# A Fourier and Hyena encoder layer on one core: data sums of the gates and of the last projection made beside the filters, weight-sum transfers one per convolution step, eight plain gate products

## The chip, the cores and the metric

The kernel runs on one core of one Trainium2 chip. The metric is the device time of one execution in microseconds, lower is better. PE is the matrix engine, DVE and ACT the vector and scalar engines, POOL the general engine, which also issues one kind of DMA, SP the engine that issues most DMAs. PSUM is the memory that PE writes, SBUF the working memory.

## What is computed

Two sequences (prompt and sample, b = 0 and 1), each 1024 positions by 1024 channels, go through the same layer, all in float32:

```python
xn = rmsnorm(x, g_pre)
fv, fg, hv, hg, mg = split(xn @ w_in)            # 8 sections of 1024 columns
fz = real(fft2 of fv over positions and groups of 256 channels)
y_f = (fz * silu(fg)) @ w_fourier_out
v, x1, x2 = split(short_conv(hv))                # width 3, per channel
z = v
for n, gate in enumerate((x1, x2)):
    z = gate * long_conv(z, filter[n])           # by FFT; filters from a small network
y_h = (z * silu(hg)) @ w_hyena_out
g_f, g_h = split(sigmoid(mg + b_merge))
out = (g_f * y_f + g_h * y_h) @ w_out
return x + rmsnorm(out, g_post)
```

The kernel keeps float32 accuracy by splitting each operand of a product into a rounded part h (made on ACT) and a remainder l (a subtraction on DVE or POOL), and by three matmuls per product: h.h, h.l, l.h (`split`, L167; `mm3`, L469; `times`, L1108).

## The kernel before

**Stages.** The Fourier branch comes first (`phase_fourier`, L601), for b = 0 and then b = 1. It also writes the normalized input of both sequences, transposed, to DRAM (`d_x`, eight blocks of 128 x 1024 each). Then `phase_main` (L986) makes 16 Hyena filters, two per block of 128 channels (`filter_taps`, `filter_spectrum`), and writes their spectra to `d_k`. Beside the filters PE gets plain gate products of b = 0 (`spill_gate`, L876), spread over the 16 filter steps by the list `fill`. Then `branches` (L1034) runs 32 convolution steps, 16 per sequence: the input product of the step (`inproj`, L838), a forward transform, the product with the spectrum, an inverse transform (`conv_back`, tables `cinv`), and the gating product on DVE (`gate`, L980), whose result is z. `phase_tail` (L1147) does what is left: gates of b = 1, the two output networks of both sequences, and the last projection with the norm.

**Plain and block products.** A plain product of 128 columns is 48 matmuls of 512 columns. `inproj` loads the weights in halves, ACT makes wh and POOL makes wl (L854), both with three buffers; for b = 1 the split weights of three sections come back from DRAM. In the tail, products go two column blocks at a time by a Strassen-like scheme with seven block products of 12 matmuls instead of eight (`PH`, L1254). For this it needs sums of weight blocks (A: 11, 12, s1 to s4, 22) and sums of data blocks (Y: B11, B21, B22 plain, T1 to T4 sums). `part2` (L1528) gives the order within a job: 11, 12 (in `first`, L1218), then s2 x T2, s3 x T3, s1 x T1, then 11 and 12 of the next job, s4 x B22, 22 x T4.

**Which gates are plain.** `PLAIN` (L1123) lists ten (section, column block) pairs of b = 1 that are done plainly: six during the last four convolution steps (L1094), and the rest after the last inverse transform (L1103, held behind `self.ended`, the last pT matmul). All other gates of b = 1 become block jobs of two column blocks, eleven of them (`gates`, L1153).

**The data sums.** At the start of the tail's gates (L1509 to L1518) the blocks of `d_x[1]` are loaded again into the raw tile (two buffers, L1511), three DVE operations per pair of row blocks make T1 to T4, and 16 splits round them. The sums of `w_out` for the last projection are made during gate jobs 2 to 5 by `last_sums` (L1241), on POOL and DVE, and stored in `d_t`; `load_sum` and `round_z` (L1399, L1404) fetch and round them at the end of the networks. A copy of `w_out` is made by eight DRAM-to-DRAM transfers on SP (L1524) to `d_wo`, from which `load_own` (L1392) reads the blocks B11, B21, B22.

**The weight sums.** `weight_sums` (L1125) makes the seven weight combinations of both networks in DRAM with 22 transfers on POOL; nine of them add into their destination (`accum_op=ADD`), and must wait for the transfer before. `front` (L1048) issues two per step, from step 2 on.

**Order of work.** The framework's planner orders the instructions of each engine by priority (order in the code) on a modelled timeline, so an instruction without a dependency may be issued much earlier than its place in the code. `issue_after(ins)` keeps the instructions of a block behind `ins` on the engine of `ins`. In the networks and at their end, functions are queued with due times in matmul-group steps (`at(t, f, ...)`, L1367; 28 steps per network, four networks), and `step` runs what is due.

**Rooms.** Memory of a stage is reused by the next one as its tiles come free. The four T tiles (16 KB per partition each) lie where the convolutions' tiles were.

Of the kernel before, what the change touches and what calls it, by code (L numbers as in the profile page):

```python
# [160 lines left out]
class K:  # L161
# [34 lines left out]
    def setup(self, ctx):  # L196
# [30 lines left out]
        self.d_t = [[dt(f"d_t{j}_{k}", [P, 512]) for k in range(4)] for j in range(4)]  # L227
# [758 lines left out]
    def phase_main(self, nct=8, nb=NB, nf=16):  # L986
        tc, nc, a = self.tc, self.nc, self.a
        with ExitStack() as es:
# [25 lines left out]
            rates = self.filter_rates(1, 0, ws)  # L1014
            for i in range(nf):
                nxt = self.filter_taps((i + 1) % 2, (i + 1) // 2, rates, ws) if i + 1 < nf else None
                self.filter_spectrum(i % 2, i // 2, taps, ws)
                if i + 2 < nf:
                    rates = self.filter_rates(i % 2, i // 2 + 1, ws, self.rounded)
                taps = nxt  # L1020
                for sec, c in fill[i * len(fill) // nf:(i + 1) * len(fill) // nf]:
                    self.spill_gate(0, sec, c, ws)
                if i == 2:
                    self.cinv = mi.tile([P, 2, INVW], F32R, name="cinv")
                    self.cin0 = mi.tile([P, 4 * P], F32, name="cin0")
                    nc.sync.dma_start(self.cin0, a["c_in0"])
                if i in (2, 4, 6):

                    s = slice((2, 4, 6).index(i) * INVW // 3, ((2, 4, 6).index(i) + 1) * INVW // 3)
                    nc.gpsimd.dma_start(self.cinv[:, :, s], a["c_inv"][:, :, s])  # L1030
            self.sums_due = list(self.weight_sums())
            self.branches(nb, nct, ws)

    def branches(self, nb, nct, ws):  # L1034
# [49 lines left out]
        for i, (b, n, c) in enumerate(steps):  # L1084
# [38 lines left out]
    PLAIN = [(5, 0), (5, 1), (6, 0), (6, 1), (5, 2), (5, 3), (6, 2), (6, 3), (5, 4), (5, 5)]  # L1123

    def weight_sums(self):  # L1125

        nc, a = self.nc, self.a
        out = []
        for n, w in enumerate(("w_fo", "w_ho")):
            v = a[w].rearrange("(j i) p (h c) -> i h p j c", i=2, h=2)  # L1130
            d = self.d_s[n]
            load = lambda p, src, d=d: out.append(lambda: nc.gpsimd.dma_start(d[p], src))
            more = lambda p, src, d=d: out.append(lambda: nc.gpsimd.dma_start(d[p], src, accum_op=ADD))
# [10 lines left out]
            more(4, v[0, 1])  # L1144
        return out

    def phase_tail(self):  # L1147
# [10 lines left out]
        with ExitStack() as es:  # L1158
# [7 lines left out]
            def prepare(nm, s, c):  # L1166
# [50 lines left out]

            def first(A, Y):  # L1218
                pa, pb = self.psum("mm", 4, "pg"), self.psum("X", 2, "pg")
# [21 lines left out]
            def last_sums(k):  # L1241
                ra, rb = [cell(xp, f"x1{2 * (k % 2) + i}", f"ws{i}") for i in range(2)]
                for r, kk in ((ra, k), (rb, 4 + k)):
                    nc.sync.dma_start(flat(r), a["w_out"][kk * P:(kk + 1) * P])
                self.sub("pool", ra[:, 0], ra[:, 0], ra[:, 1])
                self.sub("pool", ra[:, 1], ra[:, 1], rb[:, 1])
                self.stt("dve", rb[:, 1], ra[:, 0], -1.0, rb[:, 1], MUL, SUB)
                self.add("pool", rb[:, 0], rb[:, 1], rb[:, 0])
                for j, t in enumerate((ra[:, 0], rb[:, 1], ra[:, 1], rb[:, 0])):
                    nc.sync.dma_start(self.d_t[j][k], t)  # L1250
# [31 lines left out]
            def block(g, i):  # L1282
# [8 lines left out]
                if i == 0:  # L1291
                    blocks[g] = gs.tile([P, 2, 4, 512], F32R, tag=ROOM[(g - 1) % 4], name="n", bufs=1)
# [105 lines left out]

            def load_sum(nm):  # L1399
                t = Z[nm] = gs.tile([P, 2, 4, 512], F32R, tag=nm, name=f"o{nm}", bufs=1)  # L1400
                for k in range(4):
                    nc.sync.dma_start(t[:, 1, k].bitcast(F32), self.d_t[int(nm[1]) - 1][k])

            def round_z(nm, k):  # L1404
# [3 lines left out]
                else:  # L1408
                    v = t[:, 1, 2 * k:2 * k + 2]
                    self.split(t[:, 0, 2 * k:2 * k + 2], v, v.bitcast(F32), "dve", "act")  # L1410
            for nm, room, t in (("B21", "x1{}", 88), ("B11", "x0{}", 98), ("B22", "x1{}", 110)):
                at(t, load_own, nm, room)
            at(100, load_sum, "T4")
            at(104, load_sum, "T2")
            at(108, load_sum, "T3")
            for k in range(4):
                at(92 + k, round_z, "B21", k)
                at(100 + k, round_z, "B11", k)
            for k in range(2):
                at(103 + k, round_z, "T4", k)  # L1420
                at(107 + k, round_z, "T2", k)
# [86 lines left out]
            order = ("T2", "T3", "T1", "T4")  # L1508
            T = {j: gs.tile([P, 2, 4, 512], F32R, tag=j, name=j, bufs=1) for j in order}  # L1509
            for k in range(4):  # L1510
                r = gr.tile([P, 4, 512], F32, tag="raw", name="xraw", bufs=2)  # L1511
                for i in range(2):
                    nc.sync.dma_start(flat(r[:, 2 * i:2 * i + 2]), self.d_x[1][k + 4 * i])
                self.sub("dve", r[:, 0:2], r[:, 0:2], r[:, 1::2])
                self.stt("dve", r[:, 3], r[:, 0], -1.0, r[:, 3], MUL, SUB)
                self.add("dve", r[:, 2], r[:, 3], r[:, 2])
                for j, q in zip(order, (3, 1, 0, 2)):
                    self.split(T[j][:, 0, k], T[j][:, 1, k], r[:, q], "dve", "act")  # L1518
            pairs = lambda z: [(t[:, 0], t[:, 1]) for t in z]
            quad = lambda t: [(t[:, 0, k], t[:, 1, k]) for k in range(4)]  # L1520
            for j in order:
                Y[j] = quad(T[j])
            for k in range(8):
                nc.sync.dma_start(self.d_wo[k], a["w_out"][k * P:(k + 1) * P])  # L1524
# [15 lines left out]
            pa, pb, m1 = first(A, Y)  # L1540
            for i, job in enumerate(gates):
# [43 lines left out]
            Y["T1"] = quad(Z["T1"])  # L1585
# [111 lines left out]
```

## Time and profile before

| what | us |
|---|---|
| median of 3 runs | 2380.61 (2377.27 to 2382.72) |
| the profiled execution, its own time | 2382.25 |
| span of the profiled execution, first to last instruction | 2380.5 |
| PE busy | 2330.1 |
| DVE busy | 1973.3 |
| ACT busy | 1115.5 |
| POOL busy | 430.7 |

All stretches and starts are microseconds from the start of the span. The filters run from 254 to 692, the convolutions of b = 0 to about 1089 and of b = 1 to 1643, the last plain products to 1688, the gate jobs to about 1900, the networks to 2213, the output rows to the end. A busy PE isn't PE at its peak: matmuls overlap, so the pace is read from the starts. In the chain of waits and in the rows of a timeline, what stands in brackets is the engine's idle time ahead of the instruction and what ended it.

### The profile page before, as it was taken

What the parts mean: (1) busy time and instruction counts of PE and PEld (TensorE: products, weight loads), DVE (VectorE), ACT (ScalarE), POOL (GpSimd) and SP (SyncE); (2) the same over time, 40 slices, a digit from 0 to 9 for tenths busy, and PEclk for the clock granted to TensorE, in tenths of its full rate; (3) what the DMA queues carried; (4) which work ended last, traced back from release to release, by engine and by line L of the source; (5) the groups of instructions that cost most, each with busy time, mean ns of one, the idle gap of its engine ahead of it and who ended that gap; (6) DMA issues with size and microseconds to landing.
All of it is one profiled execution on the core that took longest, in us unless ns stands there. A gap on an engine that the chain in (4) does not pass through costs nothing.

```text
span 2380.5 us, 36106 instructions
## 1 busy us (share of the span) xinstructions
PE 2330.1 (98%) x12796; PEld 2022.8 (85%) x12796; DVE 1973.3 (83%) x3416; ACT 1115.5 (47%) x2083; POOL 430.7 (18%) x406
## 2 busy tenths in 40 slices
PE   6999999999999999999999999999999999999998
PEld 5999888888888888888889888888788888888786
DVE  7775688878889999999889999997765578778987
ACT  6555667776753333334222332323444365557443
POOL 2342322222243333221000000111300000101211
PEclk9999999999999999999999999999999999999999
DMA  9646655555578787745444444445754688988644
GB/s 318 207 148 220 189 175 166 166 178 171 176 261 272 244 251 231 222 149 195 153 147 133 133 142 144 140 142 177 264 186 161 217 267 272 262 310 258 174 160 142
DMA packets 241888, 471.31 MB, mean 198 GB/s; under 512 B 24103, under 2 KB 81801, under 8 KB 241387
## 3 DMA queue, kind: packets, MB, share of 16 engines
q1 hardware_dynamic: 217949, 398.06, 51.0%
q0 software_dynamic: 23536, 70.91, 10.4%
q8 instruction: 101, 1.65, 0.3%
q14 instruction: 81, 0.66, 0.1%
q10 hardware_dynamic: 221, 0.04, 0.0%
HBM read 322.63 MB, written 173.54 MB: 208 GB/s over the span
## 4 chain that ended last, share of the span: by engine, by line
PE 52%; DVE 3%; DMA 3%; issue 1%; ACT 0%; SPq 0%; DVEq 0%; POOL 0%; POOLq 0%; ACTq 0%
PE pin L193 17%; PE pg L193 14%; PE pn L193 10%; PE pT L193 5%; PE pX L193 5%; DMA d_m<-gt 1%; PE tph L904 1%; DMA xraw<-d_x 1%; DMA d_sh<-x 0%; DVE gt L180 0%; DMA g<-d_g 0%; DVE T L180 0%; DVE wl L180 0%; DVE xraw L180 0%; DVE r L180 0%
## 5 line engine op out<-in xcount | busy, mean ns | idle before, releaser
L193 PE MATMUL pin<-x,wh 128*128 128x512 f32 x2880 | 909.8, 391 | 2.5 <-ACT ktmp L794 2.4
L193 PEld LDWEIGHTS pin<-x,wh 128*128 128x128 f32 x2880 | 534.3, 188 | 103.4 <-ACT ktmp L794 2.6
L193 PE MATMUL pin<-x,wl 128*128 128x512 f32 x1440 | 563.2, 391 | 0.0
L180 POOL TENSOR_TENSOR wl<-wr,wh 128x512 fp32r<-128x512 f32 x132 | 224.2, 1699 | 1104.5 <-ACT wh L170 668.6
L193 PEld LDWEIGHTS pin<-x,wl 128*128 128x128 f32 x1440 | 271.0, 188 | 50.8
L193 PE MATMUL pn<-n,wh 128*128 128x512 f32 x896 | 276.4, 389 | 0.1
L193 PEld LDWEIGHTS pn<-n,wh 128*128 128x128 f32 x896 | 168.1, 188 | 35.8 <-DVE n L180 0.5
L193 PE MATMUL pn<-n,wl 128*128 128x512 f32 x448 | 174.6, 390 | 1.6 <-DVE wl L180 1.5
L180 DVE TENSOR_TENSOR t<-pX,k 128x1024 f32<-128x1024 f32 x128 | 155.4, 1214 | 8.7 <-DMA k<-d_k 5.9
L193 PE MATMUL pX<-bh,cfwd 128*128 128x256 f32 x768 | 162.4, 288 | 0.0
L193 PE MATMUL pT<-cinv,yh 128*128 128x256 f32 x768 | 146.0, 284 | 0.3 <-DVE T0s L180 0.3
L170 ACT CAST wh<-wr 128x512 fp32r<-128x512 f32 x132 | 81.6, 618 | 132.2 <-PE pin L193 90.3
L170 ACT CAST bh<-b 128x512 fp32r<-128x512 f32 x144 | 88.4, 619 | 99.3 <-DVE b L180 73.7
L193 PEld LDWEIGHTS pX<-bh,cfwd 128*128 128x128 f32 x768 | 126.4, 190 | 3.1 <-DVE t L180 0.4
L193 PEld LDWEIGHTS pT<-cinv,yh 128*128 128x128 f32 x768 | 122.6, 190 | 6.6 <-ACT sg L1080 0.7
L170 ACT CAST yh<-y 128x512 fp32r<-128x512 f32 x96 | 59.6, 620 | 144.5 <-DVE y L180 144.4
L1344 POOL DMA_DIRECT2D d_m<-gt x32 | 27.5, 861 | 471.7 <-DVE gt L180 442.1
L193 PE MATMUL pT<-cinv,yl 128*128 128x256 f32 x384 | 109.1, 284 | 0.7 <-DVE yl L180 0.6
L193 PE MATMUL pX<-bl,cfwd 128*128 128x256 f32 x384 | 109.2, 284 | 0.4 <-DVE bl L180 0.4
L180 DVE TENSOR_TENSOR bl<-b,bh 128x512 fp32r<-128x512 f32 x144 | 101.5, 709 | 0.5 <-ACT bh L170 0.5
L193 PEld LDWEIGHTS pn<-n,wl 128*128 128x128 f32 x448 | 84.1, 188 | 19.7 <-DVE wl L180 2.5
L180 DVE TENSOR_TENSOR y<-t 128x512 f32<-128x512 f32 x128 | 91.8, 717 | 5.4 <-PE pT L193 4.9
(370 smaller groups left out, 5045.8 us busy)
## 6 DMA issues: line engine op xcount, KB each, us to landing
k<-d_k SPq DMA_DIRECT2D x128, 512.0 KB, 4.1
wr<-in_w_in SPq DMA_DIRECT2D x132, 256.0 KB, 3.4
d_g<-gt SPq DMA_DIRECT2D x124, 256.0 KB, 2.7
wl<-d_s SPq DMA_DIRECT2D x56, 512.0 KB, 5.8
d_k<-kt SPq DMA_DIRECT2D x128, 128.0 KB, 2.2
d_k<-kt SPq DMA_DIRECT2D x64, 256.0 KB, 2.4
g<-d_g SPq DMA_DIRECT2D x64, 256.0 KB, 5.5
r<-d_g SPq DMA_DIRECT2D x60, 256.0 KB, 5.7
```

The lines of the kernel that those rows point to most:

```text
L170: self.rounded = nc.scalar.copy(h, src)
L180: return e.tensor_tensor(out, a, b, op=op)
L193: return self.nc.tensor.matmul(out, lhsT, rhs, start=start, stop=stop, skip_group_check=shared)
L904: nc.tensor.transpose(tp[:, q * P:(q + 1) * P], eo[:, e, q], self.ident)
L1344: nc.gpsimd.dma_start(dst, t, accum_op=ADD)
```

## The change

1. **Data sums beside the filters.** `d_t` now holds T1 to T4 for two uses, u = 0 for `d_x[1]` (gates) and u = 1 for `w_out` (last projection). A new function `block_sums` makes one of eight blocks in each of the filter steps 3 to 10, in a room that shares its memory with `cinv`; the loads of `cinv` move from the filter steps 2, 4 and 6 to steps 12 to 14. In the tail the four rooms are loaded from `d_t[0]` and rounded in halves, T2 and T3 ahead of the first product, T1 and T4 behind its copy. `last_sums` and the sums on the raw tile are gone.
2. **Weight sums.** One transfer per convolution step, each behind a copy of one column of that step's z on POOL; the eight copies of `w_out` to `d_wo` follow in the same list (30 transfers in all).
3. **Plain products.** `PLAIN` loses (5,4) and (5,5); the block jobs become twelve.
4. **First block job.** Its first product uses a "T" bank of PSUM in place of "mm", and its parts 11 and 12 lie in the tiles st0 and st1 and are split in one piece each.
5. **End of the networks.** The blocks of the last projection change places and due times: B11 at 60 and 64 to 67 (were 98 and 100 to 103), B21 at 98 and 101 to 104, T2 at 100, T3 at 104, T1 at 108, T4 behind the first product's copy.

```diff
-        self.d_t = [[dt(f"d_t{j}_{k}", [P, 512]) for k in range(4)] for j in range(4)]
+        self.d_t = [[dt(f"d_t{u}_{j}", [P, 4, 512]) for j in range(4)] for u in range(2)]
...
+            self.due = self.weight_sums()
+            room = mi.tile([P, 2, INVW], F32, tag="cinv", name="sums", bufs=1).rearrange("p a b -> p (a b)")
+            rows = [[self.d_x[1][k][:, 512 * h:512 * h + 512] for k in range(8) for h in range(2)],
+                    [a["w_out"][k * P:(k + 1) * P, 512 * h:512 * h + 512] for k in range(8) for h in range(2)]]
             for i in range(nf):
+                if 3 <= i < 11:
+                    u, k = (i - 3) % 2, (i - 3) // 2
+                    self.block_sums(room[:, 2048 * u:2048 * u + 2048], u, k, rows[u])
...
-                if i in (2, 4, 6):
+                if 12 <= i < 15:
...
-            with tc.issue_after(self.pooled.ins):
-                for f in self.sums_due[max(2 * i - 4, 0):max(2 * i - 2, 0)]:
-                    f()
...
             z = self.gate(n, c, y, X.pop(i))
+            if self.due:
+                mark = self.wp.tile([P, 1], F32R, tag="mark", name="mark", bufs=1)
+                with tc.issue_after(nc.gpsimd.tensor_copy(mark, z[:, 0:1]).ins):
+                    self.due.pop(0)()
...
-    PLAIN = [(5, 0), (5, 1), (6, 0), (6, 1), (5, 2), (5, 3), (6, 2), (6, 3), (5, 4), (5, 5)]
+    PLAIN = [(5, 0), (5, 1), (6, 0), (6, 1), (5, 2), (5, 3), (6, 2), (6, 3)]
+
+    def block_sums(self, room, u, k, rows):
+        r = room.rearrange("p (a b) -> p a b", a=4)
+        for q in range(4):
+            self.nc.sync.dma_start(r[:, q], rows[2 * (k + 4 * (q // 2)) + q % 2])
+        self.sub("dve", r[:, 0:2], r[:, 0:2], r[:, 1::2])
+        self.stt("dve", r[:, 3], r[:, 0], -1.0, r[:, 3], MUL, SUB)
+        self.add("dve", r[:, 2], r[:, 3], r[:, 2])
+        for q, j in enumerate((0, 2, 3, 1)):
+            self.nc.sync.dma_start(self.d_t[u][j][:, k], r[:, q])
...
+        for k in range(8):
+            out.append(lambda k=k: nc.gpsimd.dma_start(self.d_wo[k], a["w_out"][k * P:(k + 1) * P]))
...
+                elif nm == "g" and (s, c) == gates[0]:
+                    for j in range(2):
+                        t = cell(gw, f"st{j}", "wa", F32R)
+                        self.split(t[:, 0], t[:, 1], r[:, j], "dve", "act")
+                        A[("11", "12")[j]] = tri(t[:, 0]), tri(t[:, 1])
...
-            ROOM = ["T2", "T3", "T1", "T4"]
+            ROOM = [0, 3, 1, 2]
...
+            def load_t(t, u, j):
+                for k in (0, 2):
+                    nc.sync.dma_start(t[:, 1, k:k + 2].bitcast(F32), self.d_t[u][j][:, k:k + 2])
+
+            def round_t(t, k):
+                v = t[:, 1, 2 * k:2 * k + 2]
+                self.split(t[:, 0, 2 * k:2 * k + 2], v, v.bitcast(F32), "dve", "act")
...
+            order = (("T2", 0), ("T3", 3), ("T1", 1), ("T4", 2))
+            rooms = [gs.tile([P, 2, 4, 512], F32R, tag=f"t{q}", name=f"room{q}", bufs=1) for q in range(4)]
             A = prepared("g", *gates[0])
+            for j, q in order:
+                load_t(rooms[q], 0, int(j[1]) - 1)
+            for j, q in order[:2]:
+                for k in range(2):
+                    round_t(rooms[q], k)
...
-            for k in range(8):
-                nc.sync.dma_start(self.d_wo[k], a["w_out"][k * P:(k + 1) * P])
...
-            pa, pb, m1 = first(A, Y)
+            pa, pb, m1 = first(A, Y, "T", 2)
+            with tc.issue_after(self.copied.ins):
+                for j, q in order[2:]:
+                    for k in range(2):
+                        round_t(rooms[q], k)
...
-                    if 2 <= i < 6:
-                        last_sums(i - 2)
...
-            for k in range(2):
-                round_z("T3", k)
-            load_sum("T1")
             with tc.issue_after(self.copied.ins):
-                list(prep)
+                load_sum("T4")
                 for k in range(2):
                     round_z("T1", k)
+                list(prep)
                 for k in range(4):
                     round_z("B22", k)
+                for k in range(2):
+                    round_z("T4", k)
```

More of the change, by code (lines that the diff above doesn't have):

```diff
@@ L1131, in weight_sums @@
             d = self.d_s[n]
-            load = lambda p, src, d=d: out.append(lambda: nc.gpsimd.dma_start(d[p], src))
-            more = lambda p, src, d=d: out.append(lambda: nc.gpsimd.dma_start(d[p], src, accum_op=ADD))
+            load = lambda p, src, d=d: put(d[p], src)
+            more = lambda p, src, d=d: put(d[p], src, accum_op=ADD)
             load(0, v[0, 0])
@@ L1291, in block @@
                 if i == 0:
-                    blocks[g] = gs.tile([P, 2, 4, 512], F32R, tag=ROOM[(g - 1) % 4], name="n", bufs=1)
+                    blocks[g] = rooms[ROOM[(g - 1) % 4]]
                 t = blocks[g]
@@ L1397, in load_own @@
                     Z[nm].append(t)
+            def load_t(t, u, j):
[4 more added lines that the diff above has]
+                self.split(t[:, 0, 2 * k:2 * k + 2], v, v.bitcast(F32), "dve", "act")
             def load_sum(nm):
-                t = Z[nm] = gs.tile([P, 2, 4, 512], F32R, tag=nm, name=f"o{nm}", bufs=1)
-                for k in range(4):
-                    nc.sync.dma_start(t[:, 1, k].bitcast(F32), self.d_t[int(nm[1]) - 1][k])
+                t = Z[nm] = rooms[{"T2": 2, "T3": 0, "T1": 3, "T4": 1}[nm]]
+                load_t(t, 1, int(nm[1]) - 1)
             def round_z(nm, k):
@@ L1502, in end_norm @@
                     close(j, q, halves, rs)
+            order = (("T2", 0), ("T3", 3), ("T1", 1), ("T4", 2))
+            rooms = [gs.tile([P, 2, 4, 512], F32R, tag=f"t{q}", name=f"room{q}", bufs=1) for q in range(4)]
             A = prepared("g", *gates[0])
             act, dve = self.rounded.ins.engine, self.left.ins.engine
+            for j, q in order:
+                load_t(rooms[q], 0, int(j[1]) - 1)
             Y = {"B11": [self.X[k][0] for k in range(4)], "B21": [self.X[4 + k][0] for k in range(4)],
                  "B22": [self.X[4 + k][1] for k in range(4)]}
[L1508 to L1518, printed above, removed]
+            for j, q in order[:2]:
+                for k in range(2):
+                    round_t(rooms[q], k)
             pairs = lambda z: [(t[:, 0], t[:, 1]) for t in z]
             quad = lambda t: [(t[:, 0, k], t[:, 1, k]) for k in range(4)]
-            for j in order:
-                Y[j] = quad(T[j])
-            for k in range(8):
-                nc.sync.dma_start(self.d_wo[k], a["w_out"][k * P:(k + 1) * P])
+            for j, q in order:
+                Y[j] = quad(rooms[q])
             gp = gt.tile([P, D], F32, name="gp")
```

44 lines of the change are left out of this document (17 added, 27 removed).

## The prediction

> **What bounds the kernel now.** I read the page's first part, then a table of stretches (wall time, then busy time and instruction count of PE, PEld, DVE, ACT and POOL, then granted clock, DMA share, GB/s), then what PE waits for.
>
> ```profile
> span 2380.5 us, 36106 instructions
> ...
> PE 2330.1 (98%) x12796; PEld 2022.8 (85%) x12796; DVE 1973.3 (83%) x3416; ACT 1115.5 (47%) x2083; POOL 430.7 (18%) x406
> ```
>
> ```profile
> 0.00:59.51 59.51, 37.45 (x211) 31.67 (x212) 43.03 (x90) 40.71 (x72) 14.90 (x31) 0.91 0.93 318
> ...
> 324.60:536.10 211.50, 211.50 (x1177) 184.94 (x1176) 181.24 (x417) 150.50 (x324) 45.35 (x28) 1.00 0.55 171
> ...
> 691.80:1088.80 397.00, 392.98 (x2321) 346.31 (x2320) 378.15 (x590) 140.17 (x256) 135.16 (x147) 1.00 0.74 229
> 1088.80:1643.10 554.30, 554.25 (x3313) 492.67 (x3312) 509.46 (x839) 171.64 (x310) 24.90 (x14) 1.00 0.45 145
> ...
> 1688.20:1706.10 17.90, 13.00 (x43) 9.79 (x43) 13.90 (x16) 6.61 (x12) 8.37 (x6) 0.81 0.97 356
> ...
> 2195.00:2225.00 30.00, 25.07 (x102) 19.71 (x101) 25.07 (x33) 15.80 (x23) 6.55 (x8) 0.94 1.01 275
> ```
>
> ```profile
> PE tpx L359 <- DVE x L344: 11.0, 1, 11.0
> ...
> PE phd L295 <- DMA hd_w<-in_filt_w: 4.0, 1, 4.0
> PE pg L193 <- ACT m L1215: 3.7, 1, 3.7
> PE pg L193 <- DVE wl L180: 3.4, 1, 3.4
> ```
>
> The reader is to see that PE is the bound nearly everywhere: in the filter stretch (324.6 to 536.1) and in the second sequence's convolutions (1088.8 to 1643.1) it has no idle time worth naming. An edit there can only change the number of matmuls, or make PE wait where it doesn't now. PE loses time in four places: the first 60 us (59.51 - 37.45 = 22.1 us), the first sequence's convolutions (4.0 us), and the two joins of the tail, at 1688 (plain products to block products) and at 2200 (networks to output rows). A join costs more than its idle time, since the granted clock is below 1 there: at 1688 it is 4.9 us idle and 0.19 x 17.9 = 3.4 us of clock, **8.3 us**; at 2200 it is 4.9 and 0.06 x 30 = 1.8, **6.7 us**.
>
> The same in order of time (start, length, engine, line, matmul, count, idle before):
>
> ```profile
> 1688.24 0.39 PE L193 MATMUL pin<-x,wl 128*128 128x512 f32 x1
> 1689.84 0.74 PE L193 MATMUL pg<-x,wh 128*128 128x512 f32 x2 [1.21 <-ACT gt L885]
> ...
> 1695.18 0.39 PE L193 MATMUL pg<-x,wl 128*128 128x512 f32 x1
> 1699.27 1.22 PE L193 MATMUL pg<-T,s2h 128*128 128x512 f32 x2 [3.70 <-ACT m L1215]
> ...
> 1705.41 0.40 PE L193 MATMUL pg<-T,s3l 128*128 128x512 f32 x1
> ```
>
> ```profile
> 2213.70 2.88 PE L193 MATMUL pg<-oB,w 128*128 128x512 f32 x12
> 2216.43 0.61 PE L193 MATMUL pg<-oB,wh 128*128 128x512 f32 x2
> 2220.43 0.50 PE L193 MATMUL pg<-oB,wl 128*128 128x512 f32 x1 [3.39 <-DVE wl L180]
> ```
>
> Twelve matmuls in 2216.43 - 2213.70 = 2.73 us make **0.2275 us each**. After the 1.21 us gap they keep that pace; after the 3.70 us gap the 14 matmuls from 1699.27 to 1705.41 take 0.44 us each, so that gap cost about 3.0 us more than itself. The Trainium skill ("TensorE: Matmul & The Clock Gate", Part 1) says that half rate lasts one window of about 3.4 us; by that, as an estimate from the page, this gap would cost 1.7 us beside itself and the first join 7.0 us, so the forecast would be 1.3 us later. The trace has 6.1 us of slow matmuls, and the sum goes by the trace.
>
> **The change, part by part.**
>
> *Eight plain products.* Sections (5,4) and (5,5) leave the plain path, 2 x 48 = 96 matmuls of 512 columns, and become a twelfth block job of 7 x 12 = 84. Twelve fewer at 0.2275: **-2.7 us**. The job's DVE and ACT work lies beside products.
>
> *The first join.* This piece of the chain that ended last shows why T2 was late:
>
> ```profile
> 1642.08 1.21 PE pT L193 x10
> ...
> 1649.28 1.30 DVE x L176
> 1650.59 9.14 DMA d_sh<-x
> ...
> 1663.20 4.55 DMA xraw<-d_x
> ...
> 1675.16 4.70 DMA xraw<-d_x
> ...
> 1686.61 7.88 DMA xraw<-d_x
> ...
> 1699.27 0.79 PE pg L193
> ```
>
> The last convolution's result is made at 1650.6, its store lands at 1659.7, and only then a T tile may be written. After that four rounds of load, three DVE sums and four roundings follow, one round every 12 us, since the raw tile has two buffers. The change deletes the rounds: eight 512 KB loads go straight into the four rooms, and T2 and T3 need four roundings ahead of their products. A half costs:
>
> ```profile
> L170 ACT CAST oT<-oT x8: 1028/1045/1052, 2190.5 to 2221.7; 128x1024 fp32r<-128x1024 f32 x8
> L180 DVE TENSOR_TENSOR oT<-oT x8: 1214/1218/1219, 2198.9 to 2229.4; 128x1024 fp32r<-128x1024 f32 x8
> ```
>
> Against it: the cover after the last pT shrinks from four plain products to two, 96 x 0.2275 = 21.8 us. With the 24 matmuls of 11 and 12 (5.5 us), PE asks for T2 at 1643.3 + 27.3 = 1670.6 on this trace's clock. If room 0 is free once the last result is made (1650.6), a load as slow as the slowest above (7.9, or 9.1 like the store) lands by 1660, and two halves take 1.05 + 2 x 1.22 = 3.5 us: T2 at 1663, 7 us early, T3 2.4 us behind it. If room 0 must wait for the store as well, T2 comes at 1659.7 + 7.9 + 3.5 = 1671.1, half a microsecond late, too short to bring the slow matmuls. T1 and T4 are rounded behind the first copy, with 8 us and more of products ahead of their use. The other wait (1.21 us, for the last plain product's PSUM buffer) goes too: the first product takes another bank, and its weights another tile. **-8.0 us**; bounds -8.3 and, with T2 and T3 both late by 2 us, -6.
>
> *The second join.* Its start is one load:
>
> ```profile
> 2198.31 0.69 DVE L180 TENSOR_TENSOR wsum<-wraw 128x512 f32<-128x512 f32 x1 [5.50 <-DMA wraw<-d_m]
> ```
>
> DVE stands 5.5 us behind a load that landed late while the DMA share was 1.01, and works the backlog off for 25 us; both PE stalls wait for a DVE remainder. The change takes four loads and four roundings (B11) out of this stretch, into steps 60 to 67, and puts T4 behind the first product's copy. The wait itself isn't edited; it depends on where the planner sets that sum. Between 0 and -6.7, **-4.0 us**.
>
> *The copies of w_out.* Eight transfers, written in the tail's code, were issued here:
>
> ```profile
> 8.78 5.67 SPq L1524 DMA_DIRECT2D d_wo<-in_w_out  x6
> ```
>
> They read and write 4.2 MB each way, 8.4 of the 18.9 MB (318 GB/s x 59.5 us) moved in the first slice, where the DMA share is 0.93. They now go out on POOL beside the convolutions. PE's 22.1 us there are mostly not DMA: 11.0 wait for a DVE scaling, 4.0 for the very first load, before these copies. Of the other 7.1 I take **-1.0 us** (bounds -7.1 and 0).
>
> *Weight sums one per step, and the mark.* POOL's queue was held by its own accumulating transfers:
>
> ```profile
> 935.91 1.21 POOL L1133 DMA_DIRECT2D d_s<-in_w_ho  x1 [13.48 <-DMA d_s<-d_s]
> 936.60 1.84 POOL L180 TENSOR_TENSOR wl<-wr,wh 128x512 fp32r<-128x512 f32 x1
> ```
>
> At one per step (some 28 us) the previous transfer has landed, so such waits go, but each transfer now follows a one-column copy that waits for the step's gate result on DVE. Behind it in POOL's queue stand the weight remainders wl for the next input products, and PE waits for those. What covers it:
>
> ```profile
> 946.92 0.63 PE L193 MATMUL pin<-x,wh 128*128 128x512 f32 x2
> ```
>
> This is the half that uses the wl of 936.60: made at 938.4, 8.5 us early although POOL had been held 13.5 us. I take **-1.0 us** of that stretch's 4.0; bounds -4.0 and the rival below.
>
> *Sums beside the filters.* Eight blocks: four 256 KB loads, three DVE operations, four stores on SP, in filter steps 3 to 10. The same operations here:
>
> ```profile
> L180 DVE TENSOR_TENSOR xraw<-xraw 128x1024 f32<-128x1024 f32 x4 | 6.9, 1732 | 11.2 <-DMA xraw<-d_x 11.2
> L176 DVE SCALAR_TENSOR_TENSOR xraw<-xraw 128x512 f32<-128x512 f32 x4 | 3.7, 930 | 0.1
> ...
> L180 DVE TENSOR_TENSOR xraw<-xraw 128x512 f32<-128x512 f32 x4 | 2.7, 686 | 0.1
> ```
>
> That is 1.73 + 0.93 + 0.69 = 3.35 us a block, 26.8 in all (21 if the first two run at the shorter times of other rows, 1.22 and 0.69). DVE is free for 211.50 - 181.24 = 30.3 us there, so it would be 96 to 98% busy. The nearest stretch with such a DVE is 691.8 to 1088.8: 95% busy, and PE idle 1.0%. One per cent of 211.5 is **+2.0 us**; bounds 0 and 26.8 (every block delays the filter's chain in full). The tables of the inverse transform, loaded later into the same room, are first read by pT products after 691.8, some 50 us behind their load. The extra 16.8 MB raise 171 GB/s to some 250, near the 229 of the next stretch. What leaves the tail (the w_out sums on POOL and DVE, their stores) lay beside products: 0.
>
> Sum: -2.7 - 8.0 - 4.0 - 1.0 - 1.0 + 2.0 = -14.7. The profiled execution took 2382.25 us (span 2380.5), 1.6 above the median of 2380.61, so the forecast is **2367.5 us**; against the median the same sum gives 2365.9.
>
> **The rivals.**
>
> *The mark holds POOL (slower).* From the last pT (1643.3) to the result (1650.6) pass 7.3 us. If a wl stands behind the mark and PE has only the half in progress (24 x 0.2275 = 5.5 us) to cover it, PE waits 7.3 + 1.2 (issue) + 1.8 (the subtraction) - 5.5 = 4.8 us. In seven of the first sequence's sixteen steps that is 34 us: **2401 us**. It decides from the point where the hold exceeds the lead, 8.5 us in the case quoted. For it speaks that the queue is served in order, as the 13.48 us row shows; against it that PE waited for no wl of POOL's even so. The Trainium skill ("TensorE: Matmul & The Clock Gate", the table of queue depths) has GpSimd's queue strictly first in, first out; the rows agree.
>
> *DVE pays it back.* The filter steps lengthen by half of the 26.8 us, and the second join stays: -2.7 - 8.0 - 1.0 - 1.0 + 13.4 = +0.7, **2383 us**. For: 98% busy. Against: PE had no loss there at 86%, and the five steps behind the blocks can make a delay good.
>
> *The first join stays,* because 21.8 us of cover are too few or the rooms come free late: -14.7 + 8.0, **2375.5 us**. Against: the 7 us of slack above.
>
> *Nothing but the count of matmuls:* the planner moves other work into the joins, **2379.5 us**.
>
> **How the numbers follow.** Forecast 0.55, first join stays 0.12, DVE pays 0.13, only the count 0.07, the mark 0.13. A measurement of this kernel tells about 0.2% (4.8 us) from no change. The forecast and the first rival below it are faster; DVE's case is within 0.2% or, with more of the 26.8 us, above. Faster 0.67, same 0.15, slower 0.18. The range runs from 2357 (both joins and 4 us at the start gone) to 2387, the top of DVE's case with the second half of the blocks' time partly counted, and leaves out most of the mark's case. The forecast's own range is 2360 to 2374.
>
> **What would show it.** Right: no PE idle over 1 us and no clock below 1 between the last plain product and the first s3 product; PE idle under 2 us in the last networks; 12 fewer matmuls; DVE near 97% in the filter steps with PE full; no PE wait on a POOL remainder. Wrong: PE waits for wl behind a mark in the first sequence's steps; PE idle on bl, yl or kt in the filter steps; a new wait on a T tile at the first join; or a new order by the planner that puts another late load ahead of a DVE remainder.

## The result and the profile after

The changed kernel takes **2390.64 us** (median of 6 runs, 2389.58 to 2392.12), the kernel before beside it 2380.30. The ratio is 1.0044 (interval 1.0031 to 1.0056): slower by some 10 us, and outside the range of the prediction. The profiled execution took 2390.31 us.

The page's first part, and what PE waits for:

```profile
PE 2341.1 (98%) x12784; PEld 2013.8 (84%) x12784; DVE 1971.1 (83%) x3430; ACT 1110.1 (46%) x2072; POOL 452.9 (19%) x428
```

```profile
PE tpx L359 <- DVE x L344: 11.6, 1, 11.6
PE pin L193 <- DVE x L176: 7.5, 1, 7.5
...
PE pg L193 <- ACT u L1243: 1.4, 1, 1.4
PE pT L193 <- DVE T0s L180: 1.4, 1, 1.4
```

The reader is to see a contradiction. The matmuls are 12 fewer, as meant, both waits of the first join are gone, and of the 3.4 us one of the second 0.6 is left. Yet PE is busy for 11.0 us more than before (2330.1): 13.7 more than 12 fewer matmuls at 0.2275 would leave. The new wait of 7.5 us isn't in that sum, and no wait names a mark or a POOL remainder.

A table of stretches (columns as in the prediction), of before and of after:

```profile
0.00:60.00 60.00, 37.94 (x215) 32.16 (x216) 43.03 (x90) 41.20 (x72) 14.90 (x31) 0.91 0.93 318
0.00:240.00 240.00, 215.70 (x1566) 201.36 (x1567) 168.65 (x388) 138.61 (x294) 73.50 (x99) 0.98 0.65 222
...
240.00:720.00 480.00, 476.94 (x2615) 414.98 (x2614) 391.97 (x874) 316.76 (x673) 127.60 (x95) 1.00 0.59 188
720.00:1100.00 380.00, 375.98 (x2247) 332.37 (x2246) 367.59 (x568) 133.55 (x242) 123.19 (x133) 1.00 0.72 220
1660.00:1720.00 60.00, 55.10 (x230) 44.63 (x229) 42.34 (x55) 23.52 (x43) 17.54 (x13) 0.94 0.74 271
2180.00:2270.00 90.00, 85.08 (x366) 69.36 (x365) 76.16 (x123) 48.88 (x85) 21.82 (x17) 0.98 0.71 199
```

```profile
0.00:60.00 60.00, 38.61 (x256) 34.37 (x257) 44.08 (x91) 41.34 (x72) 18.33 (x31) 0.97 0.79 260
0.00:240.00 240.00, 214.21 (x1576) 200.48 (x1577) 168.85 (x388) 138.26 (x294) 76.70 (x99) 0.99 0.61 205
...
240.00:720.00 480.00, 470.97 (x2520) 400.86 (x2519) 401.41 (x881) 306.23 (x658) 132.23 (x87) 0.99 0.65 209
720.00:1100.00 380.00, 378.65 (x2248) 332.75 (x2247) 366.94 (x576) 136.30 (x246) 130.47 (x142) 1.00 0.67 203
1660.00:1720.00 60.00, 60.00 (x262) 48.84 (x262) 40.56 (x58) 29.05 (x47) 2.88 (x2) 1.00 0.70 243
2180.00:2270.00 90.00, 87.43 (x379) 70.41 (x378) 75.56 (x110) 52.34 (x86) 24.75 (x16) 1.00 0.78 225
```

The first join is gone: PE is full from 1660 to 1720 at clock 1.00 (before 4.9 us idle and 0.06 x 60 = 3.6 of clock). The filter stretch 240 to 720 lost 9.0 us of idle time where before lost 3.1. That is a loss, but it doesn't explain a PE that is busier with less work. What does is the pace, read from the starts of plain products at the same place in before and after (24 matmuls from the first row's start to the second's):

```profile
1662.63 0.62 PE L193 MATMUL pin<-x,wh 128*128 128x512 f32 x2
...
1668.07 0.62 PE L193 MATMUL pin<-x,wh 128*128 128x512 f32 x2
```

```profile
1660.04 0.63 PE L193 MATMUL pin<-x,wh 128*128 128x512 f32 x2
...
1665.64 0.63 PE L193 MATMUL pin<-x,wh 128*128 128x512 f32 x2
```

Before 5.44 / 24 = **226.7 ns**, after 5.60 / 24 = **233.3 ns**, with nothing waiting and the clock at 1.00. The groups of after by line and tile (busy us, mean ns) say which products are slow; the row ahead of them is the first group in before:

```profile
L193 PE MATMUL pin<-x,wh 128*128 128x512 f32 x2880 | 909.8, 391 | 2.5 <-ACT ktmp L794 2.4
```

```profile
L193 PE MATMUL pin<-x,wh 128*128 128x512 f32 x2816 | 901.9, 396 | 7.5 <-DVE x L176 7.5
...
L193 PE MATMUL pn<-room,wh 128*128 128x512 f32 x864 | 266.5, 389 | 0.2 <-DVE room L180 0.2
...
L193 PE MATMUL pg<-x,wh 128*128 128x512 f32 x176 | 55.3, 395 | 0.0
...
L193 PE MATMUL pg<-room,s2h 128*128 128x512 f32 x160 | 49.2, 389 | 0.0
...
L193 PE MATMUL pg<-x,s4h 128*128 128x512 f32 x96 | 29.5, 389 | 0.0
```

Data x with weights wh is slow (396 and 395, in before 391 and 390); the same x with s4h is not (389). The wh that room meets (389) is another tile of that name. So x isn't slow by itself: the **pair** is. A tile takes the same bytes in each of SBUF's 128 rows, the partitions. In the built program the weights' pool with the wh of the slow rows begins at byte 17,760 in both kernels. The first x tile lies at 40,288 before and at 40,320 after: the mark (128 x 1, but 32 bytes a partition) is the last tile of the weights' pool, and pushes all behind it by 32 bytes. The distance from the first weight tile to x was 22,528 = 11 x 2048 bytes, and is 32 more. The rooms, s4h and the other wh lie behind the mark, so these pairs moved together: slow are the products with their weights ahead of the mark and their data behind it.

### The profile page after: what moved, and what is told of

Its sections match the earlier page's. It is cut to its first block, busy times and chain, and to the rows that moved or that the text cites. A ratio compares the mean times of both kernels' runs of the same rounds, so it can differ in the third digit from the quotient of the medians.

```text
span 2388.5 us, 36189 instructions
## 1 busy us (share of the span) xinstructions
PE 2341.1 (98%) x12784; PEld 2013.8 (84%) x12784; DVE 1971.1 (83%) x3430; ACT 1110.1 (46%) x2072; POOL 452.9 (19%) x428
## 4 chain that ended last, share of the span: by engine, by line
PE 49%; issue 5%; DVE 4%; DMA 3%; POOL 0%; ACT 0%; DVEq 0%; SPq 0%; POOLq 0%; ACTq 0%
PE pin L193 19%; PE pg L193 14%; PE pn L193 5%; PE pT L193 5%; PE pX L193 5%; DMA d_m<-gt 1%; PE tph L904 1%; DVE x L176 0%; DMA oB<-d_wo 0%; DMA g<-d_g 0%; DMA k<-d_k 0%; DVE wl L180 0%; DVE t L180 0%; POOL d_m L1359 0%; DVE gt L180 0%
## 5 line engine op out<-in xcount | busy, mean ns | idle before, releaser
L193 PEld LDWEIGHTS pin<-x,wh 128*128 128x128 f32 x2816 | 523.5, 188 | 119.7 <-issue 7.6
L180 POOL TENSOR_TENSOR wl<-wr,wh 128x512 fp32r<-128x512 f32 x128 | 229.8, 1796 | 670.6 <-ACT wh L170 621.1
L193 PEld LDWEIGHTS pin<-x,wl 128*128 128x128 f32 x1408 | 265.0, 188 | 55.1
L193 PE MATMUL pn<-room,wh 128*128 128x512 f32 x864 | 266.5, 389 | 0.2 <-DVE room L180 0.2
L193 PEld LDWEIGHTS pn<-room,wh 128*128 128x128 f32 x864 | 162.1, 188 | 34.3 <-DVE room L180 0.6
L193 PE MATMUL pn<-room,wl 128*128 128x512 f32 x432 | 168.4, 390 | 0.6 <-DVE wl L180 0.5
L180 DVE TENSOR_TENSOR bl<-b,bh 128x512 fp32r<-128x512 f32 x144 | 107.1, 748 | 7.8 <-ACT bh L170 7.7
L1102 POOL CAST mark<-x 128x1 fp32r<-128x1 f32 x30 | 21.6, 720 | 411.2 <-DVE x L176 411.0
```

The source lines that it names most:

```text
L180: return e.tensor_tensor(out, a, b, op=op)
L193: return self.nc.tensor.matmul(out, lhsT, rhs, start=start, stop=stop, skip_group_check=shared)
L1102: with tc.issue_after(nc.gpsimd.tensor_copy(mark, z[:, 0:1]).ins):
```

## The experiments

Theory A: the pace depends on the distance between weights and data in SBUF, and the mark's place changed it. Theory B: the added transfers and POOL work slow the products.

**The mark's tile 128 bytes** (order of all instructions as in the changed kernel).

```diff
-                mark = self.wp.tile([P, 1], F32R, tag="mark", name="mark", bufs=1)
+                mark = self.wp.tile([P, 32], F32R, tag="mark", name="mark", bufs=1)[:, 0:1]
```

> The changed kernel with the mark tile 128 bytes long instead of 32; the order of all instructions is the same. Theory A (place): the mark is the last tile of the weights' pool, its 32 bytes move every tile behind that pool (the x tiles first) to another offset modulo 128 than the weight tiles wh and wl, and a product that reads its weights from wh or wl and its data from behind takes 0.2333 us a matmul instead of 0.2267. Then 128 bytes bring the old offset and pace back: 4680 matmuls x 0.0066 = 31 us less, about 2360. Theory B (load): the added DVE, DMA or POOL work slows the products; then the tile's length changes nothing, 2390.

Measured 2388.85 us, ratio 1.0034 (1.0021 to 1.0047). Not restored (A expected about 2360): A's guess that 128 bytes would do was wrong.

**The kernel before with 32 unused bytes behind the weights**, nothing else.

```diff
     def branches(self, nb, nct, ws):
...
+        pad = self.wp.tile([P, 1], F32, tag="pad", name="pad", bufs=1)
+        nc.gpsimd.memset(pad, 0.0)
```

> The kernel before with a 32-byte tile, cleared once and not used, as the last tile of the weights' pool; nothing else differs. Theory A: all products with weights in wh or wl take 0.2333 us, 4776 x 0.0066 = 31.5 us more, about 2412. Theory B: 2380.

Measured **2397.43 us**, ratio 1.0073 (1.0056 to 1.0090). Its page, the same count of matmuls as before:

```profile
PE 2345.9 (98%) x12796; PEld 2015.7 (84%) x12796; DVE 1969.5 (82%) x3416; ACT 1117.0 (47%) x2083; POOL 434.2 (18%) x407
...
L193 PE MATMUL pin<-x,wh 128*128 128x512 f32 x2880 | 922.3, 396 | 2.4 <-ACT ktmp L794 2.4
```

PE is busy 15.8 us more (2345.9 against 2330.1) in the work of before, and the time grows by 0.0073 x 2382 = 17 us. PE, ScalarE, VectorE and SP run the same instructions in the same order as in before. An unused tile alone brings it; B, which expected 2380, falls. The size that A expected, 31.5 us, didn't come: 6.6 ns is the difference where the products run undisturbed. Over all matmuls of x with wh or wl that follow one another directly (start to start under 300 ns), the mean rises from 228.2 to 233.1 ns. These 4.9 ns make 23 us for 4776 matmuls; why only 17 reach the time is open.

**The same tile first in the pool**, so that weights and data move together.

```diff
     def open_x(self, ctx):
...
+        pad = self.wp.tile([P, 1], F32, tag="pad", name="pad", bufs=1)
+        self.nc.gpsimd.memset(pad, 0.0)
```

> The same 32-byte tile, but as the first of the weights' pool, so that weights and data move together. Theory A, if the offset between the two counts: 2380. Theory A', if it is the data's own offset that counts (x at 0 modulo 128 instead of 96): 2412. Theory B: 2380.

Measured 2381.60 us, ratio 0.9996 (0.9985 to 1.0006); PE busy 2330.1. Absolute addresses moved, the distance didn't, and nothing changed. The first x tile lies at 40,320 here as in the changed kernel, and the first weight tile at 17,760 in before as in the changed kernel, so neither address alone makes the products slow.

**The changed kernel with a mark of 64 and of 96 bytes** (`[P, 16]` and `[P, 24]` in the line above).

> The changed kernel with a mark tile of 64 bytes, order unchanged. Theory A: if the pattern repeats every 64 bytes, fast pace and about 2360; if every 128, the pace is not 0.2267 and the time stays near 2390 or above. Theory B: 2390.

> The changed kernel with the mark's tile 96 bytes instead of 32, last in its pool: the distance between weights and data is 96 modulo 2048. Known so far from start to start: 0: 226.7 ns, 32: 233.0, 64: 228.9, 128: 232.8. If the pace goes by bit 32 of the distance (odd multiples of 32 slow), it is near 233 or above and the time 2388 to 2392; if 64 is a dip of its own between slow places on both sides, the same; if the pace follows a table without such order, anything between 226.7 and 233. A pace at 229 would say that 96 goes with 64.

Measured: 64 bytes 2377.63 us, ratio 0.9981 (0.9970 to 0.9991); 96 bytes 2393.16, ratio 1.0049 (1.0031 to 1.0067). The 24 matmuls in the runs with 128, 64 and 96 bytes:

```profile
1661.69 0.62 PE L193 MATMUL pin<-x,wh 128*128 128x512 f32 x2
...
1667.27 0.62 PE L193 MATMUL pin<-x,wh 128*128 128x512 f32 x2
```

```profile
1662.72 0.62 PE L193 MATMUL pin<-x,wh 128*128 128x512 f32 x2
...
1668.22 0.62 PE L193 MATMUL pin<-x,wh 128*128 128x512 f32 x2
```

```profile
1662.86 0.62 PE L193 MATMUL pin<-x,wh 128*128 128x512 f32 x2
...
1668.46 0.62 PE L193 MATMUL pin<-x,wh 128*128 128x512 f32 x2
```

So 5.58, 5.50 and 5.60 us, or 232.5, 229.2 and 233.3 ns each. The 64-byte run lies between the two cases that were expected of it (2360, or 2390 and above); the 96-byte run came near what odd multiples of 32 led to expect.

**The mark first in the pool**: the changed kernel with the distance of before.

```diff
     def open_x(self, ctx):
...
+        self.mark = self.wp.tile([P, 1], F32R, tag="mark", name="mark", bufs=1)
...
-                mark = self.wp.tile([P, 1], F32R, tag="mark", name="mark", bufs=1)
-                with tc.issue_after(nc.gpsimd.tensor_copy(mark, z[:, 0:1]).ins):
+                with tc.issue_after(nc.gpsimd.tensor_copy(self.mark, z[:, 0:1]).ins):
```

> The changed kernel with the mark's tile allocated first in its pool instead of last: the weights' tiles and the data tiles then both lie 32 bytes further on, and their distance is 22,528 bytes again, 0 modulo 2048; the order of every instruction is that of the changed kernel. Place: a product with these weights goes back to 226.7 ns from start to start (233.0 in the changed kernel), the mean row of the convolutions' products back to about 391 from 396, and the time to between 2367 and 2374 us (4680 matmuls by 5 to 6.3 ns less than 2390.6, less what stalls give back; 4 to 8 below the 64-byte mark). Load (the added transfers and POOL's work slow the products): the pace stays at 233 and the time at 2390. What stays of the time above 2367 would be the loss in the filters and in the first join of the filters with the convolutions.

Measured **2375.20 us**, ratio 0.9969 (0.9957 to 0.9981). PE busy is 2321.3, 19.8 us less than in the changed kernel with every instruction in the same order, and the pace is that of before (5.44 us for 24):

```profile
1662.87 0.62 PE L193 MATMUL pin<-x,wh 128*128 128x512 f32 x2
...
1668.31 0.62 PE L193 MATMUL pin<-x,wh 128*128 128x512 f32 x2
```

The place of 32 bytes is worth 1.0044 - 0.9969 = 0.0075, **18 us** (14 to 22 by the two intervals), and decides the sign of the change. The time is still 1.2 us above the upper end of what was expected of it; the next runs look for the rest in the filters.

**The sums on VectorE.** In the trace of after they don't lie in steps 3 to 10: the planner has put them all at the front of the filters.

```profile
L180 DVE TENSOR_TENSOR sums<-sums x16: 675/950/1227, 259.3 to 333.5; 128x1024 f32<-128x1024 f32 x8, 128x512 f32<-128x512 f32 x8
L176 DVE SCALAR_TENSOR_TENSOR sums<-sums x8: 673/682/691, 260.5 to 330.2; 128x512 f32<-128x512 f32 x8
```

Eight at 1.22 and sixteen at 0.68 make 20.6 us. Three kernels on the one with the mark first: without these operations, with them held behind the last VectorE operation (`self.spec`) of the filter step before, and with them on GpSimd.

```diff
-        self.sub("dve", r[:, 0:2], r[:, 0:2], r[:, 1::2])
-        self.stt("dve", r[:, 3], r[:, 0], -1.0, r[:, 3], MUL, SUB)
-        self.add("dve", r[:, 2], r[:, 3], r[:, 2])
```

> As the run with the mark first, and the three VectorE operations of each block of sums are left out: the rows are stored as they were loaded, so that the factors of the gates and of the last projection aren't made and the output isn't the reference's; every load, store and matmul stays. If VectorE's work for the sums makes the loss in the filters and the 7.5 us stall at 684 us, the time is 8 to 12 us below the run with the mark first and the stall is back to about 2.4. If the transfers or the place of the inverse tables do it, the time is within 2 us of the run with the mark first.

```diff
+                    with tc.issue_after(self.spec.ins):
-                    self.block_sums(room[:, 2048 * u:2048 * u + 2048], u, k, rows[u])
+                        self.block_sums(room[:, 2048 * u:2048 * u + 2048], u, k, rows[u])
```

> As the run with the mark first, and the three VectorE operations of each block of sums are held behind the last VectorE operation of the filter step before, so that they lie in steps 3 to 10 as the text of the change has them, instead of all within 252 to 334 us. If the loss in the filters (+2.5 and +1.4 us in two stretches of 60 us and a stall of 7.5 us at 684 us before the first convolution product, against 2.4 before) comes from where these operations stand on VectorE, the stall and the loss shrink and the time is 4 to 10 us below the run with the mark first. If it comes from the work itself (24 operations beside a VectorE that is full in these steps) or from the transfers, the time is the same within 3 us, or above it, as each step then waits for VectorE by what its sums take.

```diff
-        self.sub("dve", r[:, 0:2], r[:, 0:2], r[:, 1::2])
-        self.stt("dve", r[:, 3], r[:, 0], -1.0, r[:, 3], MUL, SUB)
-        self.add("dve", r[:, 2], r[:, 3], r[:, 2])
-        for q, j in enumerate((0, 2, 3, 1)):
+        self.sub("pool", r[:, 3], r[:, 1], r[:, 3])
+        self.sub("pool", r[:, 1], r[:, 0], r[:, 1])
+        self.sub("pool", r[:, 0], r[:, 3], r[:, 0])
+        self.add("pool", r[:, 2], r[:, 0], r[:, 2])
+        for q, j in enumerate((1, 0, 3, 2)):
```

> As the run with the mark first, and the 24 VectorE operations of the sums beside the filters become 32 GpSimd operations of 128x512 (four subtractions and additions in place for each block, some 1.9 us each by the rounding row of GpSimd, so some 60 us of an engine that is 20 to 40% busy there). If VectorE's time is what the sums cost, the time is that of the run without the VectorE sums, 2363 to 2367 us (0.7% below the kernel before), and the stall of 7.5 us before the first convolution product goes. If the two engines hold one another up when both work, or GpSimd's queue becomes late for the weights' rounding behind it, it stays at 2370 or above.

Measured: without, **2364.59 us**, ratio 0.9929 (0.9917 to 0.9940); spread, **2370.40**, 0.9953 (0.9941 to 0.9965); on GpSimd, 2381.95, 1.0002 (0.9994 to 1.0011). The stretches of the filters, with the mark first, without the sums, and spread:

```profile
240.00:360.00 120.00, 117.17 (x604) 99.47 (x603) 93.42 (x176) 67.20 (x138) 38.03 (x22) 1.00 0.91 307
360.00:660.00 300.00, 299.37 (x1670) 261.63 (x1669) 259.04 (x604) 211.12 (x462) 78.88 (x45) 1.00 0.57 178
660.00:720.00 60.00, 52.54 (x288) 45.53 (x287) 50.23 (x104) 30.13 (x62) 19.85 (x23) 0.94 0.60 194
```

```profile
240.00:360.00 120.00, 116.00 (x621) 100.04 (x621) 89.09 (x190) 76.42 (x161) 32.30 (x21) 1.00 0.93 312
360.00:660.00 300.00, 297.11 (x1654) 259.71 (x1653) 258.25 (x592) 215.84 (x461) 76.60 (x45) 1.00 0.55 174
660.00:720.00 60.00, 60.00 (x324) 51.84 (x323) 45.74 (x93) 25.82 (x53) 19.70 (x25) 1.00 0.70 226
```

```profile
240.00:360.00 120.00, 120.00 (x639) 103.70 (x638) 88.70 (x193) 75.28 (x160) 32.02 (x19) 1.00 0.57 180
...
660.00:720.00 60.00, 50.66 (x269) 43.72 (x269) 51.62 (x112) 29.82 (x65) 19.16 (x16) 0.94 0.55 178
```

The VectorE operations cost 0.9969 - 0.9929 = 0.0040, 9.5 us (some 5 to 14 by the two intervals). Where they stand PE hardly misses them: in 240 to 360 it is idle for 2.8 us with them and 4.0 without. VectorE falls behind, and PE meets that at the end, between 660 and 720, as 7.5 us idle and 3.6 of clock, which is nothing without them. What VectorE loses isn't only the operations' own 20.6 us: with the mark first it also stands idle for 9.6 us in front of them, until their loads have landed.

```profile
DVE sums L180 <- DMA sums<-d_x: 6.2, 2, 4.7
...
DVE sums L180 <- DMA sums<-in_w_out: 3.4, 2, 1.9
```

The run without the sums takes away both, so it doesn't part work from waiting. The idle time at the front goes with the transfers packed into some 80 us from 252 on (312 and 307 GB/s) or the order that came with them, which both kernels have there and before hasn't: without the sums, VectorE waits 6.4 us there for the filters' own stores (`d_k<-kt`), and in before it doesn't. Spread, with 180 GB/s, PE is full there (120.00 of 120) and no wait of VectorE for these loads is left. The end is no better for the spreading (9.3 idle, 3.6 of clock). The time is 3.8 us lower by the ratios (0.0016), but the intervals overlap, so what the place of the sums costs isn't settled.

GpSimd was no refuge. VectorE's own operations beside the sums, first with the sums on VectorE, then on GpSimd (busy us, mean ns):

```profile
L180 DVE TENSOR_TENSOR acc<-acc,ex 128x512 f32<-128x512 f32 x9 | 6.1, 679 | 0.0
```

```profile
L180 DVE TENSOR_TENSOR acc<-acc,ex 128x512 f32<-128x512 f32 x9 | 11.4, 1270 | 2.7 <-ACT ex L756 2.6
...
L180 DVE TENSOR_TENSOR T<-pft,ex 128x512 f32<-128x512 f32 x12 | 8.2, 680 | 0.4 <-ACT ex L753 0.4
```

An addition of two SBUF operands takes 1270 ns where it took 679, while `T<-pft,ex`, which reads one of its operands from PSUM, keeps its 680 (682 with the sums on VectorE). The Trainium skill ("SBUF — State Buffer", Who interferes with whom) says that a VectorE instruction with two SBUF inputs contends with a GpSimd instruction that reads SBUF; the trace agrees. PE then loses 13 us of idle time and 0.06 x 120 = 7.2 of clock at the front:

```profile
240.00:360.00 120.00, 106.80 (x532) 91.37 (x531) 104.00 (x159) 65.13 (x138) 79.27 (x51) 0.94 0.85 276
```

**The copies of w_out alone**: the kernel before with the eight d_wo transfers at the end of POOL's list.

```diff
+        for k in range(8):
+            out.append(lambda k=k: nc.gpsimd.dma_start(self.d_wo[k], a["w_out"][k * P:(k + 1) * P]))
...
-            for k in range(8):
-                nc.sync.dma_start(self.d_wo[k], a["w_out"][k * P:(k + 1) * P])
```

> One part alone: the kernel before with the eight copies of the last projection's weights moved from SP's queue at 8.8 us to the end of POOL's list beside the convolutions; nothing else changes. If these copies are what the first 60 us gained in the changed kernel (matmul loss 18.0 to 12.6 us), the time is 4 to 6 us below the kernel before. By the prediction's step (estimate 1.0) it is 0 to 1.5 below. If the start gained from something else of the change, it is the same within 1 us.

Measured 2376.05 us, ratio 0.9976 (0.9967 to 0.9985): **5.7 us** (3.6 to 7.9). Its first stretches:

```profile
0.00:60.00 60.00, 39.03 (x254) 34.69 (x255) 44.25 (x91) 41.49 (x72) 18.34 (x31) 0.94 0.81 261
0.00:240.00 240.00, 214.98 (x1579) 201.77 (x1580) 168.68 (x388) 138.22 (x295) 77.81 (x99) 0.99 0.61 205
```

PE has done 254 matmuls by 60 us (215 before), and 1579 by 240 (1566). Thirteen more at the stretch's mean of 215.70 / 1566 = 0.138 us are 1.8 us: most of the early gain is given back by 240 us. Another part shows at the first join:

```profile
1688.24 0.80 PE L193 MATMUL pg<-x,wh 128*128 128x512 f32 x2 [4.51 <-ACT gt L885]
...
1695.44 0.62 PE L193 MATMUL pg<-T,s2h 128*128 128x512 f32 x2
...
1700.88 0.62 PE L193 MATMUL pg<-T,s1h 128*128 128x512 f32 x2
```

The wait ahead of the first gate product is longer (4.51 us, before 1.21), but the one of 3.70 for T2 and the slow matmuls behind it are gone. From the start of the first wait to the first s1 product (1707.72 before) pass 17.2 us against 19.1, so 1.9 less. Why the join changed, and where the rest of the 5.7 comes from, isn't shown.

**Two transfers per step instead of one behind a mark**, on the kernel with the sums on GpSimd.

```diff
+            with tc.issue_after(self.pooled.ins):
+                for f in self.due[max(2 * i - 4, 0):max(2 * i - 2, 0)]:
+                    f()
...
-            if self.due:
-                with tc.issue_after(nc.gpsimd.tensor_copy(self.mark, z[:, 0:1]).ins):
-                    self.due.pop(0)()
```

> As the run with the sums on GpSimd, and the marks are left out: the weight-summing transfers are issued two per convolution step behind the last rounding of the gates' weights, as in the kernel before. The change's step (one per step behind a mark) was put at 1.0 us, bounds 0 to 4.0; the traces show 6.6 us of matmul loss between 780 and 1020 us in the kernel before and about 2 to 4.5 with marks. If that comes of the marks, this run is 2 to 4.5 us above the run with the sums on GpSimd. If the marks only hold GpSimd up, it is the same within 1 us, or below.

Measured 2385.47 us, ratio 1.0013 (1.0003 to 1.0023), against 1.0002 (0.9994 to 1.0011): 3.5 us by the medians in favour of the marks, but the intervals overlap. It speaks against a cost of the marks, and leaves the size of their gain open.

## Why the prediction was wrong, by its own steps

- **The pace, the step that failed.** "An edit there can only change the number of matmuls, or make PE wait where it doesn't now" left out a third way: the matmuls themselves can become slower. "Twelve matmuls in 2.73 us make 0.2275 us each" was used for all that comes after, as if a product's pace belonged to its shape. The part on the mark priced its wait, and not its 32 bytes. Some 4,700 matmuls with x or oB as data and weights of that pool became slower, by 6.6 ns each where nothing else limits them: 18 us in the time, by the run with the mark first. None of the rivals had it.
- **Sums beside the filters, mis-sized.** +2.0 was taken from the idle share of another stretch; with the mark first, 240 to 720 loses 14.5 us of idle and clock (2.8 + 0.6 + 7.5 + 3.6) where before lost 3.1: +11.4; leaving out VectorE's operations gives 9.5 back in the time. The sum of their times (21 us at the shorter rows) was right, but the planner put them at the front, not in steps 3 to 10, and the wait for their loads wasn't priced. The rival in which DVE pays it back, with half of 26.8 us, came nearest in size (13.4), but its second join, which stays, didn't come. "The five steps behind the blocks can make a delay good" was wrong: with the sums at the front more steps lay behind them, and the delay still reached PE at 660 to 720.
- **The copies of w_out.** -1.0 was taken for the first 60 us, and 5.7 measured alone, within the bounds (-7.1), but in part at the first join, which the term didn't mean. At the start the traces scatter too much to tell: by 240 us the kernel with the mark first has done 1569 matmuls, 3 more than before, or 0.4 us; the changed kernel, with the same order, 1576. All ten traces with the copies late lie between 1564 and 1585 (mean 1576), the three with them early between 1566 and 1573 (mean 1569): 7 matmuls, or 1.0 us.
- **First join, -8.0: right.** 1660 to 1720 went from 4.9 us idle and 3.6 of clock to nothing.
- **Second join, -4.0: about right.** With the mark first, 2180 to 2270 has 86.52 us busy at clock 1.00 against 85.08 at 0.98: 1.4 of idle and 1.8 of clock, -3.2.
- **Count, -2.7: right** in the matmuls, 12,784 against 12,796.
- **Weight sums, -1.0, and the rival that the mark holds POOL.** The rival didn't come: this row of after, POOL's waits, has 411 us behind marks, and PE waits for no remainder in the convolutions.

```profile
POOL mark L1102 <- DVE x L176: 411.0, 23, 41.2
```

The idle time of 720 to 1100 went from 4.0 to 1.4 us (1.8 with the mark first, so -2.2), more than the 1.0 taken; the run with two per step doesn't settle it.

The terms as the mark-first traces have them, -2.7 - 8.5 - 3.2 - 0.4 - 2.2 + 11.4, make -5.6; that kernel gained 0.0031 x 2382 = 7.4. So the forecast of -14.7 would have been 7 us too low even at the old pace (the filters' term alone is 9.4 off, and others came out a little better), and the shift of 32 bytes took 18 more.

The fastest version that makes all the sums is the changed kernel with the mark first and the sums spread: 2370.40 us, 0.5% below before.

## What to carry to other kernels

After an edit that adds or resizes any tile, compare the start-to-start time of each kind of product, tile pair by tile pair, before looking for waits; a PE that is busier with fewer matmuls is the sign. Small tiles go where they don't shift a pair of operands against each other. Work added to an engine that is full on both sides isn't hidden by the neighbour's lead: look for its price at the end of the stretch, where the lead runs out, and moving it to GpSimd can slow VectorE instead.

## What was not expected of the hardware

The pace of a 512-column float32 product depends on where its weights and its data lie relative to each other. By what the distance in bytes has over a multiple of 512:

| distance | ns a matmul | run |
|---|---|---|
| 0 | 226.7 | before; mark first |
| 32 | 233.3 | after |
| 64 | 229.2 | mark of 64 bytes |
| 96 | 233.3 | mark of 96 bytes |
| 128 | 232.5 | mark of 128 bytes |

Moving both by 32 bytes changes nothing. Multiples of 512 don't count here: a weight tile holds four blocks of 512 bytes, one for each matmul, so single matmuls of x with wh or wl lie 0, 512, 1024 or 1536 bytes modulo 2048 apart in before. The mean start-to-start times (under 300 ns) of the four groups are 228.1 to 228.3 ns; in after, 32 further, they are 233.0 to 233.2. Other distances weren't tried, and why 64 bytes cost less is open. One row of the run with the 96-byte mark doesn't fit:

```profile
L193 PE MATMUL pg<-x,s4h 128*128 128x512 f32 x96 | 30.0, 393 | 0.0
```

Both tiles lie behind the mark, their distance is a multiple of 512 as in after, and yet the mean is 393 ns where it was 389. So the distance isn't all that counts; the rest is open. The Trainium skill ("TensorE: Matmul & The Clock Gate", Part 2, Step-by-step) says that TensorE has two independent read ports, and that "Loading the next tile's weights doesn't steal SBUF read bandwidth from the running matmul." Here something that hangs on both addresses takes 2.9%, and the measurement decides; whether it is the weight load that meets the data's reads is an inference, since no run took the loads away.
